# The expert part as one list of steps with a stated order, splits three groups ahead

## The chip, the cores and the metric

The kernel runs on one core of one Trainium2 chip. The metric is the device time of one execution in microseconds (us); less is better. Three runs of the kernel before gave 1487.68, 1487.93 and 1492.42 us.

## What is computed

A two-layer decoder trunk on 256 tokens of width 1024: attention and a dense SwiGLU, then a gated linear recurrence and a mixture of experts. The change touches the last part alone:

```
logits = t @ w_router                       # t: 256 x 1024 after RMSNorm, 8 experts
top_vals, top_idx = top_k(logits, 2); top_w = softmax(top_vals)
for e in range(8):                          # w_gate, w_up: 1024 x 3584; w_down: 3584 x 1024
    y = (silu(t @ w_gate[e]) * (t @ w_up[e])) @ w_down[e]
    out = out + gates[:, e:e+1] * y
```

All weights and results are float32. Each expert's weights are read once: 8 x 3 x 1024 x 3584 x 4 bytes, 352 MB.

## The kernel before

A float32 product is made of three fp32r matmuls: each operand is split into a high part and a low rest, and `mm3` (L100) adds high x high, high x low and low x high in PSUM (lines L101, L102, L103). The activations are split when they are made. The weights have to be split on the way: `load` (L82) brings 1 MB of weights into one of 14 `raw` buffers over SP's DMA queue, and `split` (L88) makes from each half of it `w_hi` on ACT (ACTIVATE, Copy) and then `w_lo` on DVE (raw minus `w_hi`). `w_hi` and `w_lo` have four buffers each (`NSUB` = 4). A split of 128x1024 elements feeds one group of six matmuls of 512 columns.

The experts are taken in pairs. For a pair, one-hot matrices (`one_hot`, L1084) pick up to 128 tokens for each of the two experts, `gather_pair` (L1111) gathers their rows by matmul into `xgh`/`xgl` (32 matmuls of 256 columns, evictions shared by ACT and DVE), and `pair_rows` makes gates and row numbers. An expert's 3584 hidden columns are done in seven jobs of 512 (class `Job`, L1134), 56 jobs in all. A job has four parts:

- `gate` (L1160): two loads, four splits, 24 matmuls into a PSUM bank `acc`, then Silu on ACT (`sg`, L1163)
- `up` (L1165): the same 24 matmuls with the other weights, then a product on DVE (`hm`, L1168)
- `turn` (L1170): four transposes of `hm` on PE into `tp` (L1173), then the high part `hh` on ACT (L1177) and the rest `hl` on DVE (L1178); `hh` and `hl` have one buffer each
- `down` (L1180): two loads, four splits, 24 matmuls into the two PSUM banks `pj`, which collect over the seven jobs of an expert

`run_jobs` (L1258) traces them in the order gate of job n, turn of job n-1, up of job n, down of job n-1. Ahead of a new pair (`fresh`) come the gather, with the turn of the last job in its middle, and the down of the last job. When an expert is done, `add` (L1194) scales `pj` by the gates on ACT (`y`, L1202) and an indirect DMA adds the rows to `out`; these steps wait in the list `later`, which `into` (L1144) works off after its splits. `FirstJob` (L1227) computes its gate for all tokens while the routing (`route`, L1026) is under way; `LastJob` (L1214) does its down in column halves so that the first half can leave early.

The order in which an engine executes its instructions is fixed when the program is built. A planner goes through the traced instructions with its own model of their times and puts an instruction on an engine when it reckons it ready; among ready ones the earlier traced goes first. `tc.issue_after(i)` adds an edge by which the instructions of a block come behind instruction `i` on `i`'s engine; it adds no wait between engines. In the kernel before, the expert part has such edges for the `y` steps alone; where splits, Silu, `hh`, `hl`, `hm`, transposes and matmuls stand against each other is the planner's choice. Each engine works through its own list in order.

Of the kernel before, what the change touches and what calls it, by code (L numbers as in the profile page):

```python
# [16 lines left out]
P = 128  # L17
D = 1024
KT = D // P
NT = 2  # L20
# [19 lines left out]
def tile_trunk(  # L40
# [59 lines left out]
    def mm3(ps, xh, xl, wh, wl, first, last, chk=False):  # L100
        nc.tensor.matmul(ps, lhsT=xh, rhs=wh, start=first, stop=False, skip_group_check=chk)  # L101
        nc.tensor.matmul(ps, lhsT=xh, rhs=wl, start=False, stop=False, skip_group_check=chk)  # L102
        nc.tensor.matmul(ps, lhsT=xl, rhs=wh, start=False, stop=last, skip_group_check=chk)  # L103
# [1007 lines left out]
    def gather_pair(oneh, between=None):  # L1111

        xg = slot_tiles(2 * P)
        for k0 in range(0, KT, 2):
            if k0 == 4 and between:
                between()
            for src, dst in ((nh, xg[0]), (nl, xg[1])):
                pt = bank("acc", 4)
                for i in range(2):
                    k = k0 + i  # L1120
                    for t in range(NT):
                        nc.tensor.matmul(pt[:, i * 256:(i + 1) * 256], lhsT=src[t][:, k * P:(k + 1) * P],
                                         rhs=oneh[:, t], start=(t == 0), stop=(t == NT - 1))
                pv = pt.rearrange("p (a b) -> p a b", b=256)
                if src is nh:
                    nc.scalar.activation(dst[:, k0:k0 + 2], pv, AF.Copy)
                else:
                    nc.vector.tensor_copy(dst[:, k0:k0 + 2], pv)
        return xg

    NCH = FE // 512
    later = []

    class Job:  # L1134
# [9 lines left out]
        def into(self, w):  # L1144
            rows = self.rows()
            ps = [bank("acc", 4) for _ in rows]
            for k0 in (0, 4):
                r = load([4, 512], lambda r: [(r, w[:, k0:k0 + 4, self.ch * 512:(self.ch + 1) * 512])])
                for i in range(0, 4, 2):
                    wh, wl = split(r[:, i:i + 2], [2, 512])  # L1150
                    for j in range(2):
                        k = k0 + i + j
                        for p_, (xh, xl, es) in zip(ps, rows):
                            mm3(p_, xh[:, k, es], xl[:, k, es], wh[:, j], wl[:, j], k == 0, k == KT - 1)
                    if later and k0 + i:
                        with tc.issue_after(split.last[0].ins):
                            later.pop(0)()
            return ps

        def gate(self):  # L1160
            ps, = self.into(self.wg)
            self.sg = moe.tile([P, 512], F32, name="sg", tag="sg", bufs=1)
            nc.scalar.activation(self.sg, ps, AF.Silu)  # L1163

        def up(self):  # L1165
            ps, = self.into(self.wu)
            self.hm = moe.tile([P, 512], F32, name="hm", tag="hm", bufs=1)
            nc.vector.tensor_mul(self.hm, ps, self.sg)  # L1168

        def turn(self):  # L1170
            pt = bank("tp")
            for i in range(4):
                nc.tensor.transpose(out=pt[:, i * P:(i + 1) * P], in_=self.hm[:, i * P:(i + 1) * P], identity=ident)  # L1173
            self.hh = moe.tile([P, 4, P], F32R, name="hh", tag="hh", bufs=1)
            self.hl = moe.tile([P, 4, P], F32R, name="hl", tag="hl", bufs=1)
            ptv = pt.rearrange("p (a b) -> p a b", b=P)
            nc.scalar.activation(self.hh, ptv, AF.Copy)  # L1177
            nc.vector.tensor_sub(self.hl, ptv, f32(self.hh))  # L1178

        def down(self):  # L1180
            sh, ch = self.shared, self.ch
            if ch == 0:
                sh["py"] = [bank("pj") for _ in range(2)]
            for i0 in (0, 2):
                r = load([2, D], lambda r: [(r, self.wd[:, 4 * ch + i0:4 * ch + i0 + 2, :])])
                for i in range(2):
                    wh, wl = split(r[:, i], [D])
                    for c in range(2):
                        mm3(sh["py"][c], self.hh[:, i0 + i], self.hl[:, i0 + i], wh[:, HALF[c]], wl[:, HALF[c]],
                            ch == 0 and i0 + i == 0, ch == NCH - 1 and i0 + i == 3)  # L1190
            if ch == NCH - 1:
                later.extend(self.add(0, 2, out_rows, 0))

        def add(self, c0, c1, rows, i):  # L1194

            (gate, idx), j, py = self.shared["slots"], self.slot, self.shared["py"]
            box = {}

            def scaled(c):
                if c == c0:  # L1200
                    box["y"] = lows.tile([P, 2, 512], F32, name="y", tag="low1")
                nc.scalar.activation(box["y"][:, c], py[c], AF.Copy, scale=gate[:, j:j + 1])  # L1202
                if c == c1 - 1:
                    out_of(box["y"])

            def out_of(y):
                nc.gpsimd.indirect_dma_start(
                    out=rows, out_offset=bass.IndirectOffsetOnAxis(ap=idx[:, i, j:j + 1], axis=0),
                    in_=y[:, c0:c1].rearrange("p a b -> p (a b)"), in_offset=None, bounds_check=rows.shape[0] - 1,
                    oob_is_err=True, compute_op=ALU.add)  # L1210

            return [lambda c=c: scaled(c) for c in range(c0, c1)]

    class LastJob(Job):  # L1214

        def down(self):
            sh = self.shared
            for c in range(2):
                for i0 in (0, 2):
                    r = load([2, 512], lambda r: [(r, self.wd[:, 4 * self.ch + i0:4 * self.ch + i0 + 2, HALF[c]])])  # L1220
                    wh, wl = split(r, [2, 512])
                    for i in range(2):
                        mm3(sh["py"][c], self.hh[:, i0 + i], self.hl[:, i0 + i], wh[:, i], wl[:, i], False, i0 + i == 3)
                for step in self.add(c, c + 1, out_halves, 1 + c):
                    step()

    class FirstJob(Job):  # L1227

        def gate(self):
            self.ch_rows = [(*dense, TOK[t]) for t in range(NT)]  # L1230
            self.sgh = lows.tile([P, NT, 512], F32R, name="sgh", tag="low1")
            self.sgl = []
            for t, ps in enumerate(self.into(self.wg)):
                sg = moe.tile([P, 512], F32, name="sg", tag=("sg", "hm")[t], bufs=1)
                nc.scalar.activation(sg, ps, AF.Silu, scale=rx[t])
                nc.scalar.activation(self.sgh[:, t], sg, AF.Copy)
                self.sgl.append(moe.tile([P, 512], F32R, name="sgl", tag=("hl", "hh")[t], bufs=1))
                nc.vector.tensor_sub(self.sgl[t], sg, f32(self.sgh[:, t]))
            self.ch_rows = None
# [4 lines left out]
        def up(self):  # L1244
            sh = self.shared
            sh["oneh"] = one_hot(0)
            sh["xg"] = gather_pair(sh["oneh"])
            sh["slots"] = pair_rows(sh["oneh"], 0)
            pt = bank("tp")
            for t in range(NT):  # L1250
                for n, part in enumerate((self.sgh[:, t], self.sgl[t])):
                    nc.tensor.matmul(pt, lhsT=sh["oneh"][:, t, 0], rhs=part, start=(t == 0 and n == 0),
                                     stop=(t == NT - 1 and n == 1))
            self.sg = moe.tile([P, 512], F32, name="sg", tag="sg", bufs=1)
            nc.scalar.activation(self.sg, pt, AF.Copy)
            super().up()

    def run_jobs(jobs):  # L1258

        prev = None  # L1260
        for job in jobs + [None]:
            if job and job.fresh:
                job.fresh(job.shared, prev.turn)
                prev.down()
                prev = None
            if job:
                job.gate()
            if prev:
                prev.turn()
            if job:  # L1270
                job.up()
            if prev:
                prev.down()
            prev = job

    jobs = []
    for e in range(NE):
        if e % 2 == 0:
            shared = {}

            def fresh(sh, between, e=e):
                sh["oneh"] = one_hot(e)
                sh["xg"] = gather_pair(sh["oneh"], between)
                sh["slots"] = pair_rows(sh["oneh"], e)
# [9 lines left out]
    run_jobs(jobs)  # L1294
# [7 lines left out]
    with tc.If(most > P):  # L1302
        ecur = mc.tile([P, 1], F32, name="ecur")
        nc.vector.memset(ecur, 0.0)
        with tc.For_i(0, NE, 1) as e:
# [27 lines left out]
            run_jobs([Job(ch, shared, slice(0, P), ws, 0) for ch in range(NCH)])  # L1333
            while later:
                later.pop(0)()
# [44 lines left out]
```

## Time and profile before

| | us |
|---|---|
| three runs: lowest, median, highest | 1487.68, 1487.93, 1492.42 |
| the profiled execution, its own time | 1489.99 |
| its span, first to last instruction | 1488.3 |
| PE busy, over the span | 1453.3 (98%) |
| DVE busy, over the span | 1213.9 (82%) |
| ACT busy, over the span | 1035.2 (70%) |
| first expert gather matmul | at 510.7 |
| down part of the first job begins | at 532.81 |
| down part of the last job but one begins | at 1464.62 |

How to read it: matmuls are pipelined, each row of PE lasts longer than the distance to the next, so PE shows as busy throughout and busy time doesn't tell whether it ran at its best. The distance from one start to the next does. PEld is the weight load of a matmul; its idle time has a releaser when it waited for another engine. A row of the timeline gives start, length, engine, line, operation, what it writes and reads, how many rows were merged, and in brackets the idle time just before it and what ended it.

### The profile page before, as it was taken

The page shows a single profiled execution, that of the slowest core. Times are in us where ns is not written, and L with a number is a line of the kernel's source. Part 1 is how long each engine was busy: PE and PEld are TensorE (multiplying, and loading weights), DVE is VectorE, ACT ScalarE, POOL GpSimd, SP SyncE. Part 2 cuts the span into 40 slices and gives each one's busy share as a digit, 9 for nine tenths or more (in the row PEclk, how much of TensorE's full clock was granted, in tenths as well). Part 3 has the DMA queues.
Part 4 walks back from the last instruction along what each step waited for, and adds up shares of the span by engine and source line. Part 5 has one row for each costly group of instructions (what it writes and reads, how often), then busy time and mean ns, then how long its engine had stood idle before and what let it go on. Part 6 is the DMA issues. An engine that isn't in the chain of part 4 may idle for free.

```text
span 1488.3 us, 20143 instructions
## 1 busy us (share of the span) xinstructions
PE 1453.3 (98%) x7509; PEld 1216.6 (82%) x7509; DVE 1213.9 (82%) x1460; ACT 1035.2 (70%) x1285; POOL 31.9 (2%) x45
## 2 busy tenths in 40 slices
PE   7999999999999999999999999999999999999996
PEld 6887899998889788888888878888877888887885
DVE  7775656557867899999989888889888888888885
ACT  6655544445766688888878777777777777778774
POOL 1000000000000100000000000000000000000000
PEclk9999999999999999999999999999999999999999
DMA  9933355656454499999999999999999999999971
GB/s 315 369 125 114 128 182 187 186 183 183 142 170 142 143 348 365 384 370 385 379 348 376 356 351 395 360 353 360 374 367 373 381 366 350 356 371 362 391 262 16
DMA packets 209691, 434.05 MB, mean 292 GB/s; under 512 B 7402, under 2 KB 58642, under 8 KB 209586
## 3 DMA queue, kind: packets, MB, share of 16 engines
q1 hardware_dynamic: 207506, 425.77, 79.6%
q0 software_dynamic: 2080, 6.92, 2.3%
q8 instruction: 61, 1.00, 0.3%
q14 instruction: 44, 0.36, 0.1%
HBM read 427.41 MB, written 5.24 MB: 291 GB/s over the span
## 4 chain that ended last, share of the span: by engine, by line
issue 53%; PE 37%; DMA 5%; DVE 2%; ACT 2%; POOL 0%; SPq 0%; POOLq 0%; ACTq 0%; DVEq 0%
PE acc L101 5%; PE acc L102 5%; PE acc L103 5%; DMA out_dram<-y,idx 4%; PE pj L342 3%; PE pj L344 3%; PE pj L343 3%; PE pj L101 2%; PE pj L103 2%; PE pj L102 2%; DVE w_lo L91 1%; PE pj L760 1%; PE pj L761 1%; PE pj L762 1%; PE tp L556 1%
## 5 line engine op out<-in xcount | busy, mean ns | idle before, releaser
L91 DVE TENSOR_TENSOR w_lo<-raw,w_hi 128x1024 fp32r<-128x1024 f32 x810 | 956.8, 1221 | 169.2 <-ACT w_hi L91 153.5
L91 ACT ACTIVATE w_hi<-raw 128x1024 fp32r<-128x1024 f32 x810 | 830.0, 1057 | 248.4 <-PE acc L103 82.9
L102 PE MATMUL acc<-w_lo,xgh 128*128 128x512 f32 x904 | 357.9, 396 | 0.0
L101 PE MATMUL acc<-w_hi,xgh 128*128 128x512 f32 x904 | 354.2, 392 | 1.0 <-ACT xgh L294 1.0
L103 PE MATMUL acc<-w_hi,xgl 128*128 128x512 f32 x904 | 353.2, 391 | 0.0
L102 PEld LDWEIGHTS acc<-w_lo,xgh 128*128 128x128 f32 x904 | 169.6, 188 | 51.8 <-DVE w_lo L91 14.6
L101 PEld LDWEIGHTS acc<-w_hi,xgh 128*128 128x128 f32 x904 | 169.8, 188 | 37.1 <-ACT xgh L294 1.2
L103 PEld LDWEIGHTS acc<-w_hi,xgl 128*128 128x128 f32 x904 | 169.8, 188 | 33.0
L102 PE MATMUL pj<-w_lo,hh 128*128 128x512 f32 x448 | 177.8, 397 | 0.0
L103 PE MATMUL pj<-w_hi,hl 128*128 128x512 f32 x448 | 174.9, 390 | 0.0
L101 PE MATMUL pj<-w_hi,hh 128*128 128x512 f32 x448 | 158.1, 391 | 0.7 <-ACT hh L1177 0.5
L101 PEld LDWEIGHTS pj<-w_hi,hh 128*128 128x128 f32 x448 | 84.1, 188 | 19.6 <-ACT hh L1177 0.9
L103 PEld LDWEIGHTS pj<-w_hi,hl 128*128 128x128 f32 x448 | 84.2, 188 | 16.3
L102 PEld LDWEIGHTS pj<-w_lo,hh 128*128 128x128 f32 x448 | 84.2, 188 | 16.3
L342 PE MATMUL pj<-xh,w_hi 128*128 128x256 f32 x320 | 90.8, 284 | 0.6 <-DVE hm L677 0.6
L343 PE MATMUL pj<-xl,w_hi 128*128 128x256 f32 x320 | 90.5, 283 | 0.0
L344 PE MATMUL pj<-xh,w_lo 128*128 128x256 f32 x320 | 90.5, 283 | 0.0
L1163 ACT ACTIVATE sg<-acc 128x512 f32<-128x512 f32 x55 | 32.9, 598 | 52.8 <-PE acc L103 52.8
L1177 ACT ACTIVATE hh<-tp 128x512 fp32r<-128x512 f32 x56 | 33.4, 596 | 49.8 <-PE pj L102 43.4
L342 PEld LDWEIGHTS pj<-xh,w_hi 128*128 128x128 f32 x320 | 61.4, 192 | 1.2 <-DVE hm L677 0.8
L343 PEld LDWEIGHTS pj<-xl,w_hi 128*128 128x128 f32 x320 | 61.4, 192 | 0.4
L344 PEld LDWEIGHTS pj<-xh,w_lo 128*128 128x128 f32 x320 | 61.4, 192 | 0.0
(300 smaller groups left out, 1594.3 us busy)
## 6 DMA issues: line engine op xcount, KB each, us to landing
raw<-in_moe_w_gate_dram SPq DMA_DIRECT2D x112, 1024.0 KB, 7.4
raw<-in_moe_w_up_dram SPq DMA_DIRECT2D x112, 1024.0 KB, 7.9
raw<-in_moe_w_down_dram SPq DMA_DIRECT2D x110, 1024.0 KB, 7.6
raw<-in_ffn_w_gate_dram SPq DMA_DIRECT2D x22, 512.0 KB, 3.8
raw<-in_ffn_w_up_dram SPq DMA_DIRECT2D x22, 512.0 KB, 4.8
raw<-in_ffn_w_down_dram SPq DMA_DIRECT2D x11, 1024.0 KB, 4.8
raw<-in_hgrn_w_in_dram SPq DMA_DIRECT2D x10, 1024.0 KB, 5.5
raw<-in_attn_w_in_dram SPq DMA_DIRECT2D x16, 512.0 KB, 9.3
```

The lines of the kernel that those rows point to most:

```text
L91: split.last = nc.scalar.activation(hi, view, AF.Copy), nc.vector.tensor_sub(lo, view, f32(hi))
L101: nc.tensor.matmul(ps, lhsT=xh, rhs=wh, start=first, stop=False, skip_group_check=chk)
L102: nc.tensor.matmul(ps, lhsT=xh, rhs=wl, start=False, stop=False, skip_group_check=chk)
L103: nc.tensor.matmul(ps, lhsT=xl, rhs=wh, start=False, stop=last, skip_group_check=chk)
L342: nc.tensor.matmul(o, lhsT=wh[:, i, j], rhs=xh[:, k], start=k == 0 and j == 0, stop=False, skip_group_check=True)
L343: nc.tensor.matmul(o, lhsT=wh[:, i, j], rhs=xl[:, k], start=False, stop=False, skip_group_check=True)
L344: nc.tensor.matmul(o, lhsT=wl[:, i, j], rhs=xh[:, k], start=False, stop=k == KT - 1, skip_group_check=True)
L556: nc.tensor.matmul(po[:, j * 64:(j + 1) * 64], lhsT=pT[:, kb, j, :], rhs=v[:, kb, j * 64:(j + 1) * 64], start=(j == 0 and kb == 0), stop=( ...
L760: nc.tensor.matmul(o, lhsT=wh[:, k], rhs=xh[:, k], start=first, stop=False, skip_group_check=True)
L761: nc.tensor.matmul(o, lhsT=wh[:, k], rhs=xl[:, k], start=False, stop=False, skip_group_check=True)
L1163: nc.scalar.activation(self.sg, ps, AF.Silu)
L1177: nc.scalar.activation(self.hh, ptv, AF.Copy)
```

## The change

The jobs no longer issue their work part by part. Each part returns a list of steps, `order` strings the lists of all jobs together in the same sequence as `run_jobs` did, and `run` issues the one list. A step is either a plain function or a `Split`, which has a load, a view of it, and `use`, the matmuls of the group. Before `run` issues the matmuls of a group it issues the splits up to three groups further (`AHEAD = NSUB - 1`), across the borders of parts and jobs. `tails` holds the last instruction issued on PE, ACT and DVE; `in_turn` puts every following split, group of matmuls, Silu, `hm`, `turn`, gather step and `y` behind these, each engine on its own. `one_hot` of a new pair is traced behind the gate of the last job before it, and `later` is worked off after every group. `FirstJob`'s own steps (apart from the gather), `one_hot`, `pair_rows` and the loads are in no such order. The number of matmuls, splits, loads and evictions, the tiles and the buffers stay as they are.

```diff
+    tails = {}
+    @contextmanager
+    def in_turn():
+        with ExitStack() as st:
+            for i in tails.values():
+                st.enter_context(tc.issue_after(i.ins))
+            yield
+    AHEAD = NSUB - 1
+    class Split:
+        def __init__(self, load_, view, shape, use):
+            self.load, self.view, self.shape, self.use = load_, view, shape, use
+        def ready(self):
+            with in_turn():
+                self.parts = split(self.view(self.load()), self.shape)
+            tails["act"], tails["dve"] = split.last
+    def run(steps):
+        splits = [x for x in steps if isinstance(x, Split)]
+        n = done = 0
+        for x in steps:
+            if not isinstance(x, Split):
+                x()
+                continue
+            while n < min(len(splits), done + AHEAD + 1):
+                splits[n].ready()
+                n += 1
+            with in_turn():
+                tails["pe"] = x.use(*x.parts)
+            done += 1
+            if later:
+                later.pop(0)()
...
         def into(self, w):
-            rows = self.rows()
-            ps = [bank("acc", 4) for _ in rows]
-            for k0 in (0, 4):
-                r = load([4, 512], lambda r: [(r, w[:, k0:k0 + 4, self.ch * 512:(self.ch + 1) * 512])])
-                for i in range(0, 4, 2):
-                    wh, wl = split(r[:, i:i + 2], [2, 512])
...
+            return [Split(ld, lambda r, i=i: r[:, i:i + 2], [2, 512], lambda wh, wl, k=k0 + i: use(k, wh, wl))
+                    for k0, ld in ((0, part(0)), (4, part(4))) for i in (0, 2)]
...
         def turn(self):
             pt = bank("tp")
+            with in_turn():
+                for i in range(4):
+                    tails["pe"] = nc.tensor.transpose(out=pt[:, i * P:(i + 1) * P], in_=self.hm[:, i * P:(i + 1) * P], identity=ident)
...
+                tails["act"] = nc.scalar.activation(self.hh, ptv, AF.Copy)
+                tails["dve"] = nc.vector.tensor_sub(self.hl, ptv, f32(self.hh))
...
+    def order(jobs):
+        steps, prev = [], None
+        for n, job in enumerate(jobs):
+            if job.fresh:
+                a, b = gather_steps(job.shared)
+                steps += [a, prev.turn, b, lambda job=job: job.fresh(job.shared)] + prev.down()
                 prev = None
+            steps += job.gate()
+            if n + 1 < len(jobs) and jobs[n + 1].fresh:
+                steps.append(jobs[n + 1].one_hot)
             if prev:
+                steps.append(prev.turn)
+            steps += job.up()
             if prev:
+                steps += prev.down()
             prev = job
+        return steps + [prev.turn] + prev.down()
```

## Rows read from the trace of the kernel before

**Rows 1.** Page, part 1: busy us, share of the span, instructions.

```profile
PE 1453.3 (98%) x7509; PEld 1216.6 (82%) x7509; DVE 1213.9 (82%) x1460; ACT 1035.2 (70%) x1285; POOL 31.9 (2%) x45
```

**Rows 2.** Busy us (instructions): PE, PEld, DVE, ACT, POOL; clock, DMA share, GB/s.

```profile
533.00:735.00 202.00, 202.00 (x915) 167.18 (x914) 187.55 (x169) 164.60 (x171) 1.69 (x1) 1.00 1.03 377
...
1259.00:1461.00 202.00, 202.00 (x900) 162.42 (x899) 178.75 (x166) 153.34 (x167) 1.83 (x1) 1.00 0.91 332
```

**Rows 3.** Timeline of PE: where six down parts, one gate and one turn begin.

```profile
532.81 0.39 PE L101 MATMUL pj<-w_hi,hh 128*128 128x512 f32 x1
...
555.06 0.39 PE L101 MATMUL acc<-w_hi,xgh 128*128 128x512 f32 x1
...
560.51 0.60 PE L1173 MATMUL tp<-ident,hm 128*128 128x128 f32 x4
...
734.45 0.39 PE L101 MATMUL pj<-w_hi,hh 128*128 128x512 f32 x1
...
772.33 0.39 PE L101 MATMUL pj<-w_hi,hh 128*128 128x512 f32 x1
...
839.79 0.62 PE L101 MATMUL pj<-w_hi,hh 128*128 128x512 f32 x2
...
856.92 0.61 PE L101 MATMUL pj<-w_hi,hh 128*128 128x512 f32 x2
...
1464.62 0.62 PE L101 MATMUL pj<-w_hi,hh 128*128 128x512 f32 x2
```

**Rows 4.** Timeline of ACT and DVE, one job of the early stretch.

```profile
560.71 0.60 ACT L1163 ACTIVATE sg<-acc 128x512 f32<-128x512 f32 x1 [0.31 <-PE acc L103]
561.20 0.59 ACT L1177 ACTIVATE hh<-tp 128x512 fp32r<-128x512 f32 x1
561.68 2.01 ACT L91 ACTIVATE w_hi<-raw 128x1024 fp32r<-128x1024 f32 x2
...
562.77 4.80 DVE L91 TENSOR_TENSOR w_lo<-raw,w_hi 128x1024 fp32r<-128x1024 f32 x4 [0.26 <-ACT w_hi L91]
...
567.49 0.68 DVE L1168 TENSOR_TENSOR hm<-acc,sg 128x512 f32<-128x512 f32 x1
```

**Rows 5.** Timeline of ACT, DVE and PE, one job of the later stretch.

```profile
897.27 0.60 ACT L1177 ACTIVATE hh<-tp 128x512 fp32r<-128x512 f32 x1 [1.45 <-PE pj L102]
...
902.95 0.60 ACT L1163 ACTIVATE sg<-acc 128x512 f32<-128x512 f32 x1 [1.30 <-PE acc L103]
...
904.53 3.50 DVE L91 TENSOR_TENSOR w_lo<-raw,w_hi 128x1024 fp32r<-128x1024 f32 x3 [1.05 <-ACT w_hi L91]
...
905.47 0.39 PE L101 MATMUL acc<-w_hi,xgh 128*128 128x512 f32 x1
905.81 0.50 PE L102 MATMUL acc<-w_lo,xgh 128*128 128x512 f32 x1
```

**Rows 6.** Waits of PEld, 822 to 1465; its groups by line, 549.6 to 734.4.

```profile
PEld acc L102 <- DVE w_lo L91: 14.6, 41, 0.4
...
L102 PEld LDWEIGHTS acc<-w_lo,xgh 128*128 128x128 f32 x176 | 33.1, 188 | 6.5
```

**Rows 7.** Timeline of ACT and PE behind the first gather between pairs.

```profile
743.86 0.60 ACT L1126 ACTIVATE xgh<-acc 128x512 fp32r<-128x512 f32 x1 [0.34 <-PE acc L1122]
...
744.51 0.48 PE L101 MATMUL pj<-w_hi,hh 128*128 128x512 f32 x1
```

**Rows 8.** Waits of SP's queue; DMA issues (KB, median us to landing), 533 to 735.

```profile
SPq L85 <- DVE w_lo L91: 171.0, 73, 3.3
...
raw<-in_moe_w_up_dram SPq DMA_DIRECT2D x24, 1024.0 KB, 8.1
```

**Rows 9.** Timeline of ACT and PE at the last turn.

```profile
1470.51 0.60 ACT L1177 ACTIVATE hh<-tp 128x512 fp32r<-128x512 f32 x1 [1.44 <-PE pj L102]
...
1471.16 0.50 PE L101 MATMUL pj<-w_hi,hh 128*128 128x512 f32 x1 [0.46 <-ACT hh L1177]
```

**Rows 10.** Timeline of PE at the first gather.

```profile
510.70 0.39 PE L1122 MATMUL acc<-oneh,nh 128*128 128x256 f32 x1 [1.30 <-DVE oneh L1087]
```

More of the change, by code (lines that the diff above doesn't have):

```diff
@@ L102, in mm3 @@
         nc.tensor.matmul(ps, lhsT=xh, rhs=wl, start=False, stop=False, skip_group_check=chk)
-        nc.tensor.matmul(ps, lhsT=xl, rhs=wh, start=False, stop=last, skip_group_check=chk)
+        return nc.tensor.matmul(ps, lhsT=xl, rhs=wh, start=False, stop=last, skip_group_check=chk)
     def pair_load(w, c0, c1, k):
@@ L1109, in pair_rows @@
         return slot_rows(lambda t, j: oneh[:, t, j], lambda t, j: info[:, t, e + j], 2)
[L1111 to L1129, printed above, removed]
+    tails = {}
@@ L1170, in turn, with out_ @@
+        def up(self):
+            def out_():
+                self.hm = moe.tile([P, 512], F32, name="hm", tag="hm", bufs=1)
+                with in_turn():
+                    tails["dve"] = nc.vector.tensor_mul(self.hm, self.ps[0], self.sg)
+            return self.into(self.wu) + [out_]
         def turn(self):
             pt = bank("tp")
-            for i in range(4):
-                nc.tensor.transpose(out=pt[:, i * P:(i + 1) * P], in_=self.hm[:, i * P:(i + 1) * P], identity=ident)
@@ L1191, in down, with use, part @@
-            if ch == NCH - 1:
-                later.extend(self.add(0, 2, out_rows, 0))
+            def use(i, wh, wl):
+                if ch == 0 and i == 0:
+                    sh["py"] = [bank("pj") for _ in range(2)]
+                for c in range(2):
+                    m = mm3(sh["py"][c], self.hh[:, i], self.hl[:, i], wh[:, HALF[c]], wl[:, HALF[c]],
+                            ch == 0 and i == 0, ch == NCH - 1 and i == 3)
+                return m
+            def part(i0):
+                return once(lambda: load([2, D], lambda r: [(r, self.wd[:, 4 * ch + i0:4 * ch + i0 + 2, :])]))
@@ L1194, in add @@
+            steps = [Split(ld, lambda r, i=i: r[:, i], [D], lambda wh, wl, i=i0 + i: use(i, wh, wl))
+                     for i0, ld in ((0, part(0)), (2, part(2))) for i in range(2)]
+            return steps + ([lambda: later.extend(self.add(0, 2, out_rows, 0))] if ch == NCH - 1 else [])
         def add(self, c0, c1, rows, i):
@@ L1216, in down, with use, leave @@
         def down(self):
-            sh = self.shared
+            sh, steps = self.shared, []
+            def use(c, i0, wh, wl):
+                for i in range(2):
+                    m = mm3(sh["py"][c], self.hh[:, i0 + i], self.hl[:, i0 + i], wh[:, i], wl[:, i], False, i0 + i == 3)
+                return m
+            def leave(c):
+                for step in self.add(c, c + 1, out_halves, 1 + c):
+                    step()
             for c in range(2):
                 for i0 in (0, 2):
[L1220 to L1225, printed above, removed]
+                    ld = once(lambda c=c, i0=i0: load([2, 512], lambda r: [
+                        (r, self.wd[:, 4 * self.ch + i0:4 * self.ch + i0 + 2, HALF[c]])]))
+                    steps.append(Split(ld, lambda r: r, [2, 512], lambda wh, wl, c=c, i0=i0: use(c, i0, wh, wl)))
+                steps.append(lambda c=c: leave(c))
+            return steps
     class FirstJob(Job):
@@ L1245, in up, with ready @@
             sh = self.shared
[L1246 to L1264, printed above, removed]
+            def ready():
+                sh["oneh"] = one_hot(0)
+                for step in gather_steps(sh):
+                    step()
+                sh["slots"] = pair_rows(sh["oneh"], 0)
+                pt = bank("tp")
+                for t in range(NT):
+                    for n, part in enumerate((self.sgh[:, t], self.sgl[t])):
+                        nc.tensor.matmul(pt, lhsT=sh["oneh"][:, t, 0], rhs=part, start=(t == 0 and n == 0),
+                                         stop=(t == NT - 1 and n == 1))
+                self.sg = moe.tile([P, 512], F32, name="sg", tag="sg", bufs=1)
+                nc.scalar.activation(self.sg, pt, AF.Copy)
+            return [ready] + super().up()
+    def order(jobs):
[4 more added lines that the diff above has]
+                steps += [a, prev.turn, b, lambda job=job: job.fresh(job.shared)] + prev.down()
                 prev = None
-            if job:
-                job.gate()
+            steps += job.gate()
+            if n + 1 < len(jobs) and jobs[n + 1].fresh:
+                steps.append(jobs[n + 1].one_hot)
             if prev:
-                prev.turn()
-            if job:
-                job.up()
+                steps.append(prev.turn)
+            steps += job.up()
             if prev:
-                prev.down()
+                steps += prev.down()
             prev = job
+        return steps + [prev.turn] + prev.down()
     jobs = []
@@ L1279, in tile_trunk, with fresh, hot @@
             shared = {}
[L1281 removed]
+            def fresh(sh, e=e):
+                sh["slots"] = pair_rows(sh["oneh"], e)
+            def hot(sh=shared, e=e):
                 sh["oneh"] = one_hot(e)
[L1283 to L1284 removed]
             if e == 0:
@@ L1293, in tile_trunk @@
                 fresh if e in (2, 4, 6) and ch == 0 else None))
-    run_jobs(jobs)
+            jobs[-1].one_hot = hot
+    run(order(jobs))
     cmax = mc.tile([P, 1], F32, name="cmax")
@@ L1332, in tile_trunk @@
             shared = dict(xg=xg2, slots=slot_rows(lambda t, j: oh2[:, t], lambda t, j: info2[:, t], 1))
-            run_jobs([Job(ch, shared, slice(0, P), ws, 0) for ch in range(NCH)])
-            while later:
-                later.pop(0)()
+            tails.clear()
+            run(order([Job(ch, shared, slice(0, P), ws, 0) for ch in range(NCH)]))
             nc.vector.tensor_scalar(ecur, ecur, 1.0, None, op0=ALU.add)
```

99 lines of the change are left out of this document (61 added, 38 removed).

## The prediction, made before the change was run

> **What bounds the kernel now.** I read the page's busy times first. PE shows 98% [rows 1], and in the expert part it shows as busy in every microsecond, at the full clock: the granted clock is 1.00 of full speed, the 2.4 GHz level, in both stretches [rows 2]. So PE sets the time there. But overlapping matmul rows hide small losses, so the next view is the timeline of PE, read by distances between starts. A gate part has 24 matmuls from 555.06 to 560.51 [rows 3]: 5.45 / 24 = 0.227 us from one to the next, without a break. A job has 72 of them, 16.34 us, and four transposes.
>
> Then I mark where each job's down part begins and compare the distances. From 532.81 to 734.45 there are twelve jobs [rows 3], 201.64 / 12 = 16.80 us each: 0.46 us above the 72 matmuls, which the transposes account for. From 839.79 to 856.92 it is 17.13 [rows 3]. So the same work runs in two ways, an early one (A) and a later one (B), and B loses about 0.3 us in each job.
>
> The waits of PEld say where: from 822 to 1465 it waited for `w_lo` 41 times, 14.6 us in all, and for nothing else; in A its weight loads of the same line have idle time but no releaser [rows 6]. One such wait is the step from 905.47 to 905.81 [rows 5], 0.34 us instead of 0.227.
>
> Last I read ACT and DVE in both. In A a job's order on ACT is Silu, `hh`, then the splits, and Silu waits 0.31 us [rows 4]; DVE does four `w_lo` before `hm`. In B the planner put `hh` before a split, although the one `hh` buffer is read by the running down part to its end: ACT stands 1.45 us until that frees it, and Silu then stands 1.30 us [rows 5]. The splits queued behind come late, DVE stands 1.05 us for `w_hi` [rows 5], and PE waits for that `w_lo`. This is a matter of order; the buffers, instructions and durations are the same in A and B.
>
> **The change, part by part.**
>
> *The list's order.* I set the list of steps against the A rows. Before the last gate group the splits up to the third group of up are issued; then Silu, the transposes, `hh`, `hl`; then the last split of up, then those of down. On ACT that gives Silu, `hh`, then splits, and on DVE `hl`, four `w_lo`, `hm`: the order of rows 4. In A every split also starts when the group before the one now running has freed its buffer, which is three groups ahead with four buffers. So the list is A for all jobs, and A's pace needs no estimate. The edges are on one engine each and cost no instruction.
>
> The price: from 532.81 to 1464.62 [rows 3] the kernel takes 931.81 us. There are 54 distances from one down part to the next; six of them lie at the three gathers between pairs, two at each. In A these two take 772.33 - 734.45 = 37.88 us [rows 3]. All in A: 48 x 16.803 + 3 x 37.88 = 806.5 + 113.6 = 920.2 us. **The gain is 931.8 - 920.2 = 11.6 us**, all of it on PE's path. A larger gain isn't there: the whole of PEld's wait is 14.6 us.
>
> *Waits in the new order.* A split that is released late now holds all that is behind it. The tightest place is the Silu: behind it stand `hh` and the last split of up. Silu starts 0.31 us after ACT fell idle, `hh` 0.49 us later, the split 0.48 us later [rows 4]; PE needs that split three groups of 1.36 us and the transposes after the gate's end at 560.51 [rows 3], at about 564.9. Its `w_lo` begins at 562.77 and takes 1.2 us [rows 4], so it is there at 564.0. That leaves 0.9 us of cover, and A shows no wait.
>
> *The loads* are issued at a split's place in the list, so up to three groups earlier in the program. They are in none of the orders; SP has been ahead by its 14 buffers anyway: it waited 171 of 202 us for a free buffer, and a load lands 8.1 us after its issue [rows 8]. Cost nothing; their cover is the lead of 14 buffers, 14 x 2.8 = 39 us of PE work at six loads to a job, less 8.
>
> *Gathers between pairs.* The list puts the last split of a job's down behind all evictions; the kernel before had it ahead of them. The last `xgh` eviction starts at 743.86 and takes 0.60 us [rows 7]. So in the list the split starts at about 744.5, its `w_lo` is ready 2.3 us later, at 746.8, and PE, which begins that down part at 744.51 [rows 7], comes to it three groups later, at 748.6. Cost nothing with 1.8 us of cover; without it up to 1 us at each of three places. `one_hot` and `pair_rows` float as before.
>
> *First job.* PE stands 1.30 us until the one-hot matrix is there [rows 10], at the end of DVE's routing work. The splits of up now precede `one_hot` in the program, but four buffers let at most three of them come early, and three have done so before. No row shows the new place: at best the 1.30 us goes, at worst three `w_lo` of 1.2 us [rows 4] come in front (3.6 us). I take 0, since the same three splits stand there before.
>
> *The end.* The last turn now follows the last but one down in full. Before, the first matmul behind that turn starts at 1471.16, 6.54 us after 1464.62 [rows 3, 9]. Now: 24 matmuls 5.44, transposes to `hh` 0.69 (560.51 to 561.20 [rows 3, 4]), `hh` to matmul 0.65 [rows 9], 6.78 us; against that, the wait for a late split that followed goes, as three are ready. I take 0, with -0.6 to +0.8.
>
> *A rule against the trace.* PE's pace in A is 0.227 us a matmul with no wait beside it [rows 3, 6]. The Trainium skill (TensorE: Matmul & The Clock Gate, section "Wait — 56ns, not 53.3ns?") has 215.7 ns from start to start for 512 columns at the full clock. By that figure a job would have 0.8 us less, and the gain would be some 45 us more; the trace doesn't agree, and the measured pace stands.
>
> **The sum.** -11.6 us. The profiled execution took 1489.99 us (its span is 1488.3), the median of the runs 1487.93, 2.06 us less. 1489.99 - 11.6 = 1478.4 as a profiled run, 1476.3 against the median, 0.8% faster.
>
> **The rivals.**
>
> *New waits eat half.* The unordered rest (`one_hot`, `pair_rows`, the first job's steps) or the gather borders add waits: 3.6 us at the first job, 1 us at each gather, together 6.6 us; 1482.9. Against it: the first gather shows no wait in nearly the same order. 8%.
>
> *It doesn't do what it says.* The planner's order stays where it matters, or the wait returns at another place in the job: 1487.9. For it speaks only that edges add order and no speed; against it that each of the instructions that stand wrongly in rows 5 is tied. 6%.
>
> *The transfers become the bound; slower.* Now DMA moves 377 GB/s in A at a share of 1.03 [rows 2], which looks full. If the core can't hold that for the rest, the 31 us of lead are used up. The point of decision: 56 jobs of 6.29 MB, less the lead, end no earlier than 931.8 + 31 us if the rate is 366 GB/s; below that the kernel is slower than before, at 355 GB/s by 992 - 963 = 29 us, 1517. Against it: landing takes 8 of 39 us, and SP waits for buffers, not for data [rows 8]. The Trainium skill (Perfetto Trace Analysis, section "Identifying the Most-Contended Engine") calls occupancy misleading for the 16 DMA engines and goes by HBM utilization; by that the share of 1.03 would be no sign of a bound, and the rows agree. 4%.
>
> *More than A.* The 1.30 us at the first job and the wait at the end go too: 1474. 4%. *The pace of the matmuls falls too*: a weight load takes 0.188 us [rows 6], so 0.227 might hold something that an order frees; each 0.01 us is 40 us in 4032 matmuls, and one such step gives 1436. No stretch of A shows it: 1%.
>
> **How the numbers follow.** The forecast gets 77%. A measurement of this kernel tells about 0.3%, 4.5 us, from no change. Faster by more than that are the forecast, the half (5.0 us), more and the pace: 77 + 8 + 4 + 1 = 90%, of which I move 2% to no change, since the half lies near the bound: 88%. Same: 6 + 2 = 8%. Slower: 4%. The range goes from 1473 (all of the bounds for the first job and the end below the forecast, 1.9 us, and the runs' spread) to 1482 (the first job's 3.6 us, the end's 0.8, and a run from the upper part of a spread of 4.7 us); it leaves out the transfers, no change and most of the half.
>
> **What would show it.** Right: down parts 16.8 us apart up to the last gather, no wait of PEld for `w_lo`, Silu and `hh` back to back on ACT in every job, DVE with four `w_lo` before `hm`, the last down but one beginning near 1453. Wrong: distances of 17.1 that stay, ACT waits of 1.3 us for Silu or `hh`, ACT waiting for `raw` or landings above 30 us (transfers), a longer wait than 1.30 us ahead of the first gather, distances over 38 us at the gathers. The prediction falls as a whole if the tied order turns out to differ from rows 4 in a place that these rows do not show.

## The result, and the profile after

The changed kernel takes 1476.61 us (median of six runs, 1475.87 to 1481.65), the kernel before 1487.93 us on the same chip: a ratio of 0.9918 with a 95% interval of 0.9903 to 0.9933, or 11.3 us less. The profiled execution took 1475.87 us, with a span of 1474.2 us.

The page's busy times can't show it; PE still stands at 98%, as in [rows 1]:

```profile
PE 1439.5 (98%) x7509; PEld 1220.1 (83%) x7509; DVE 1231.7 (84%) x1460; ACT 1059.0 (72%) x1285; POOL 32.5 (2%) x45
```

The distances do. PE's timeline of the changed kernel (start, us; duration, us; what): the first gather, the first down part, the fourth group of one at the first gather between pairs, two down parts in a row of the later stretch, the last but one, and the first matmul behind the last turn.

```profile
508.25 0.38 PE L1133 MATMUL acc<-oneh,nh 128*128 128x256 f32 x1 [1.30 <-DVE oneh L1087]
...
530.52 0.39 PE L101 MATMUL pj<-w_hi,hh 128*128 128x512 f32 x1
...
746.42 0.39 PE L101 MATMUL pj<-w_hi,hh 128*128 128x512 f32 x1
...
887.66 0.39 PE L101 MATMUL pj<-w_hi,hh 128*128 128x512 f32 x1
...
904.47 0.39 PE L101 MATMUL pj<-w_hi,hh 128*128 128x512 f32 x1
...
1450.71 0.39 PE L101 MATMUL pj<-w_hi,hh 128*128 128x512 f32 x1
...
1457.44 0.50 PE L101 MATMUL pj<-w_hi,hh 128*128 128x512 f32 x1 [0.69 <-ACT hh L1239]
```

The later stretch has 904.47 - 887.66 = 16.81 us to a job where [rows 3] has 17.13, and so has every other job down to the end; the two distances at each gather between pairs sum to 37.85, 37.85 and 37.84 us. From the first down part to the last but one it is 1450.71 - 530.52 = 920.19 us, against 931.81 in [rows 3]: 11.6 us less. Between 515 and 1455 us PEld now waits for nothing at all, where [rows 6] has 41 waits.

ACT and DVE, a job of the later stretch (this answers to [rows 5]), and three rows of ACT and DVE at the first gather between pairs:

```profile
742.07 1.05 ACT L91 ACTIVATE w_hi<-raw 128x1024 fp32r<-128x1024 f32 x1
743.34 1.22 DVE L91 TENSOR_TENSOR w_lo<-raw,w_hi 128x1024 fp32r<-128x1024 f32 x1
...
898.74 0.60 ACT L1219 ACTIVATE sg<-acc 128x512 f32<-128x512 f32 x1 [0.30 <-PE acc L103]
899.23 0.59 ACT L1239 ACTIVATE hh<-tp 128x512 fp32r<-128x512 f32 x1
899.71 2.01 ACT L91 ACTIVATE w_hi<-raw 128x1024 fp32r<-128x1024 f32 x2
...
900.80 4.83 DVE L91 TENSOR_TENSOR w_lo<-raw,w_hi 128x1024 fp32r<-128x1024 f32 x4 [0.25 <-ACT w_hi L91]
905.55 0.68 DVE L1227 TENSOR_TENSOR hm<-acc,sg 128x512 f32<-128x512 f32 x1
```

It is the order of [rows 4], to within 0.01 us: Silu 0.30 us after ACT fell idle, `hh` 0.49 us later, four `w_lo` before `hm`. ACT's waits from 533 to 1455 us (us in total, times, longest) say the same of all jobs:

```profile
ACT sg L1219 <- PE acc L103: 16.3, 54, 0.3
...
ACT hh L1239 <- PE tp L1235: 0.9, 3, 0.3
```

Two stretches, as in [rows 2] (busy us of PE, PEld, DVE, ACT, POOL; clock, DMA share, GB/s):

```profile
533.00:735.00 202.00, 202.00 (x915) 167.19 (x914) 187.75 (x170) 164.46 (x171) 1.96 (x1) 1.00 1.02 376
1245.00:1447.00 202.00, 202.00 (x915) 167.21 (x914) 187.52 (x169) 164.67 (x172) 1.82 (x1) 1.00 0.92 339
```

SP's queue, 533 to 735 us, as in [rows 8]:

```profile
SPq L85 <- DVE w_lo L91: 169.1, 72, 3.3
```

The loads of up there (KB, us to landing):

```profile
raw<-in_moe_w_up_dram SPq DMA_DIRECT2D x24, 1024.0 KB, 7.2
```

The late stretch now holds 915 matmul records in 202 us like the early one, where [rows 2] has 900. The two profiled spans differ by 14.1 us, more than the medians do; 2.4 us of that lie before 150 us, in code that the change leaves alone, where the two executions just differ: PE's last transposes ahead of the routing begin at 488.17 us here and at 490.59 us before.

### The profile page after: what moved, and what is told of

The parts are those of the page before. It is cut to its first block, busy times and chain, and to the rows that moved or that the text cites. A ratio compares the mean times of both kernels' runs of the same rounds, so it can differ in the third digit from the quotient of the medians.

```text
span 1474.2 us, 20073 instructions
## 1 busy us (share of the span) xinstructions
PE 1439.5 (98%) x7509; PEld 1220.1 (83%) x7509; DVE 1231.7 (84%) x1460; ACT 1059.0 (72%) x1285; POOL 32.5 (2%) x45
## 4 chain that ended last, share of the span: by engine, by line
issue 61%; PE 29%; DMA 5%; DVE 2%; ACT 2%; POOL 0%; SPq 0%; POOLq 0%; ACTq 0%; DVEq 0%
DMA out_dram<-y,idx 4%; PE acc L101 3%; PE acc L102 3%; PE acc L103 3%; PE pj L342 3%; PE pj L344 3%; PE pj L343 3%; PE pj L101 1%; PE pj L103 1%; PE pj L102 1%; PE pj L760 1%; PE pj L761 1%; PE pj L762 1%; DVE w_lo L91 1%; PE tp L556 1%
## 5 line engine op out<-in xcount | busy, mean ns | idle before, releaser
L91 DVE TENSOR_TENSOR w_lo<-raw,w_hi 128x1024 fp32r<-128x1024 f32 x810 | 975.1, 1223 | 156.6 <-ACT w_hi L91 116.9
L91 ACT ACTIVATE w_hi<-raw 128x1024 fp32r<-128x1024 f32 x810 | 853.5, 1062 | 299.7 <-PE acc L103 127.5
L102 PE MATMUL acc<-w_lo,xgh 128*128 128x512 f32 x904 | 352.4, 390 | 0.0
L102 PE MATMUL pj<-w_lo,hh 128*128 128x512 f32 x448 | 174.3, 389 | 0.0
L101 PE MATMUL pj<-w_hi,hh 128*128 128x512 f32 x448 | 163.5, 390 | 0.7 <-ACT hh L1239 0.7
L101 PE MATMUL acc<-w_hi,xh 128*128 128x512 f32 (+1 forms) x160 | 58.7, 368 | 1.5 <-ACT xh L294 0.8
L102 PE MATMUL acc<-w_lo,xh 128*128 128x512 f32 (+1 forms) x160 | 57.6, 361 | 0.0
```

The source lines that it names most:

```text
L91: split.last = nc.scalar.activation(hi, view, AF.Copy), nc.vector.tensor_sub(lo, view, f32(hi))
```

## The experiments

In all of them "distance" is that between the starts of two down parts in a row, and "first to last" the time from the first to the last but one; the changed kernel has 16.80 and 920.19 us.

**Lead.** The list changes two things at once: the place of the turn and of Silu, and the lead of the splits, three groups ahead of PE. These two kernels keep the list and take the lead away.

```diff
-    AHEAD = NSUB - 1
+    AHEAD = NSUB - 2
```

(ahead1 has `NSUB - 3`.)

> The changed kernel with splits issued two groups ahead instead of three; all order edges stay. Theory of place (the one of the prediction: what cost time was that hh and Silu stood too early on ACT): both still stand back to back behind the gate, so the distance between down parts stays 16.8 us and the time 1476 to 1478. Theory of lead (what cost time was that only two split groups were ready when ACT came to the Silu, so that the third one's w_lo came too late): the third split of up now stands behind Silu and hh, its w_lo is there 3.5 us after the start of the transposes and PE wants it at 0.36 + 2 x 1.36 + 0.23 = 3.3 us, so every job waits for w_lo once, some 0.3 us as before the change: distance 17.1, time 1476 + 54 x 0.3 = 1492.

> The changed kernel with splits issued one group ahead; all order edges stay. Theory of lead: at the Silu the second split of up is late by 3.5 - 0.36 - 1.36 - 0.23 = 1.6 us, and at hm the second split of down by about 0.45 us, so each job loses 2.0 us: distance 18.9, time about 1476 + 110 = 1586. Theory of place: no loss at the Silu, since its place and that of hh are unchanged; only the 0.45 us at hm, distance 17.3, time about 1500.

Two groups ahead: ratio 1.0012 (1.0002 to 1.0023), so the whole gain is gone; distances 17.05 to 17.10 us, first to last 934.4 us. One group ahead, in one run: 1591.9 us, distances 18.83 to 18.88. PE, ACT and DVE of one job of the kernel with two groups ahead show the order to be right and the loss to be there:

```profile
889.81 0.60 ACT L1219 ACTIVATE sg<-acc 128x512 f32<-128x512 f32 x1 [1.66 <-PE acc L103]
890.30 0.59 ACT L1239 ACTIVATE hh<-tp 128x512 fp32r<-128x512 f32 x1
890.78 4.90 ACT L91 ACTIVATE w_hi<-raw 128x1024 fp32r<-128x1024 f32 x5
...
891.87 4.63 DVE L91 TENSOR_TENSOR w_lo<-raw,w_hi 128x1024 fp32r<-128x1024 f32 x4 [0.25 <-ACT w_hi L91]
...
892.79 0.39 PE L101 MATMUL acc<-w_hi,xgh 128*128 128x512 f32 x1
893.15 0.50 PE L102 MATMUL acc<-w_lo,xgh 128*128 128x512 f32 x1
893.49 0.39 PE L103 MATMUL acc<-w_hi,xgl 128*128 128x512 f32 x1
```

Its waits of PEld (us in total, times, longest):

```profile
PEld acc L102 <- DVE w_lo L91: 20.9, 55, 0.4
```

One wait in each job, and always this one. The chain from Silu to the first `w_lo` is the same as in the changed kernel: 889.81 to 891.87 is 2.06 us, and so is 898.74 to 900.80. What differs is which group that `w_lo` is for. With three ahead it is the fourth group of up, with two ahead the third, which PE reaches 1.36 us sooner. It is ready at 891.87 + 1.2 = 893.1, and the weight load that waits for it would run beside the matmul of 892.79. So PE goes 0.36 and 0.34 us where 0.227 is its pace: 0.25 us lost, the whole of the longer distance.

**The turn's place.** The rival was that the place makes the gain: `hh` and Silu no longer stand in front of splits while they wait. Here the turn is put where ACT must stand for it, right behind the previous job's down, with three groups ahead as before, and then with two.

```diff
-                steps += [a, prev.turn, b, lambda job=job: job.fresh(job.shared)] + prev.down()
+                steps += [a] + ([] if prev.turned else [prev.turn]) + [b, lambda job=job: job.fresh(job.shared)] + prev.down()
...
-                steps += prev.down()
+                steps += prev.down() + [job.turn]
```

(late_turn2 has `AHEAD = NSUB - 2` on top.)

> The changed kernel with the turn of a job moved from behind the next gate to behind the down of the job before, so that on ACT hh stands ahead of the next gate's last split and waits for the end of that down, as it did in the slow stretch before the change; three groups ahead and all edges stay. Theory of place: ACT stands for hh in every job again, distance 17.1 and time 1487 to 1490. Theory of lead: three split groups are ready when ACT gets there and the split behind hh still comes 1 us early, distance 16.8, time 1475 to 1479.

> The changed kernel with the turn moved as in late_turn and splits two groups ahead: the two things that rows of the slow stretch before the change show together. Theory of lead: the slow stretch again, one wait of PEld for w_lo in each job, at the third group of up; distance 17.0 to 17.1, time 1488 to 1492. If place and lead add up: distance 17.3 or more, since Silu and hh each hold the splits at a place of their own, time above 1500.

With three ahead: 0.9917 (0.9901 to 0.9934), the same gain; first to last 921.1 us, where the 0.9 us more lie at the gathers (PEld waits 0.8 us there for `xgh`). ACT and PE of one job:

```profile
896.36 0.60 ACT L1239 ACTIVATE hh<-tp 128x512 fp32r<-128x512 f32 x1 [0.74 <-PE tp L1235]
896.85 2.00 ACT L91 ACTIVATE w_hi<-raw 128x1024 fp32r<-128x1024 f32 x2
...
901.85 0.60 ACT L1219 ACTIVATE sg<-acc 128x512 f32<-128x512 f32 x1 [0.30 <-PE acc L103]
...
907.09 0.62 PE L101 MATMUL pj<-w_hi,hh 128*128 128x512 f32 x2
...
923.88 0.61 PE L101 MATMUL pj<-w_hi,hh 128*128 128x512 f32 x2
```

ACT's wait for the turn, 533 to 1455 us:

```profile
ACT hh L1239 <- PE tp L1235: 37.7, 51, 0.7
```

ACT stands 37.7 us for `hh`, in 51 jobs, and the distance is 923.88 - 907.09 = 16.79 us. So standing in front of splits costs nothing here: the lead covers it. With two ahead, one run: 1501.9 us, distances of 17.27 to 17.32 (one in each pair 17.40 to 17.44), and the waits come twice in a job:

```profile
PEld acc L102 <- DVE w_lo L91: 38.0, 111, 0.4
```

Place and lead draw on the same cover: either fault alone costs 0 (place) or 0.26 us (lead), both together 0.5 us a job.

**The edges.** Does the list need them, or does writing the steps in this order do? And does tying the turn alone do?

```diff
-            for i in tails.values():
-                st.enter_context(tc.issue_after(i.ins))
```

> The changed kernel without the edges: the steps are traced in the same sequence with splits three groups ahead, but the planner may put them in another order. If the edges do the work: the planner falls back into the late order, with transposes in the middle of a down part and waits of PEld for w_lo, 1484 to 1488. If the sequence in which the steps are traced is enough: 1475 to 1478 and no such wait.

Ratio 1.002 (1.0009 to 1.0031), first to last 933.8 us. The distances are 16.80 up to the fourth job behind the first gather between pairs, and 17.1 from there: the place where the kernel before changes from A to B. ACT and PE of one such job:

```profile
887.11 0.60 ACT L1217 ACTIVATE sg<-acc 128x512 f32<-128x512 f32 x1 [1.30 <-PE acc L103]
887.60 4.91 ACT L91 ACTIVATE w_hi<-raw 128x1024 fp32r<-128x1024 f32 x5
...
889.97 0.50 PE L102 MATMUL acc<-w_lo,xgh 128*128 128x512 f32 x1
```

It is the sight of [rows 5]: Silu stands 1.30 us on an ACT that has no split left to do before it, then five splits in a row, and a `w_lo` matmul that comes late. Without edges the planner orders this program much as it ordered the one before.

One part of the change alone is the kernel before with its turn tied behind the next gate's last matmul and Silu:

```diff
+            self.silu = nc.scalar.activation(self.sg, ps, AF.Silu)
...
-            if prev:
+            if prev and job:
+                with tc.issue_after(job.mm.ins), tc.issue_after(job.silu.ins):
+                    prev.turn()
+            elif prev:
```

> The kernel before, with one thing of the change: the four transposes of a turn come behind the last matmul of the next gate on PE, and hh behind that gate's Silu on ACT. Splits, matmuls, Silu and hm stay with the planner, and nothing is traced ahead. If the early transposes and hh were what led the planner into the late order: distances of 16.8 throughout, no wait for w_lo, 1476 to 1479. If the splits ahead are needed: distances near 17.1 return, 1485 to 1490.

Ratio 1.0076 (1.0057 to 1.0095): slower than the kernel before, with distances of 17.45 to 17.53 in the later stretch, 944.2 us from first to last, and waits in two places:

```profile
PEld pj L102 <- DVE w_lo L91: 17.0, 33, 0.5
PEld acc L102 <- DVE w_lo L91: 14.9, 39, 0.8
```

A tied turn with splits that still float is worse than all floating, so the turn's edges alone don't carry the gain. A kernel with the edges of the splits alone was not run.

**More lead.** Five split buffers and four groups ahead; 13 load buffers instead of 14 make the room.

```diff
-NRAW = 14
-NSUB = 4
+NRAW = 13
+NSUB = 5
```

> The changed kernel with five w_hi/w_lo buffers and splits four groups ahead (13 raw buffers instead of 14, to make room). If PE is the bound with three groups ahead, more lead gives nothing: distance 16.8, 1475 to 1478. If a wait that no row shows is left in the pace of 0.227 us a matmul, a longer lead shortens it: distance below 16.7, 1470 or less.

Ratio 0.9954 (0.9941 to 0.9967): faster than the kernel before, but not as fast as with three. The distances are 16.80, and the first gather between pairs takes no longer than before. The second and third take 12.19 + 27.72 = 39.91 us instead of 37.85, together 4.1 us, which is all of 924.3 - 920.2 us. PE's longest wait from 515 us on says at what:

```profile
PE acc L1133 <- DVE xgl L1140: 2.6, 2, 1.3
```

DVE at the second gather says why:

```profile
983.30 0.17 DVE L1099 COPY sv<-tp 128x8 f32<-128x8 f32 x1 [4.30 <-PE tp L1096]
...
983.58 2.36 DVE L91 TENSOR_TENSOR w_lo<-raw,w_hi 128x1024 fp32r<-128x1024 f32 x2
985.86 1.28 DVE L1140 CAST xgl<-acc 128x512 fp32r<-128x512 f32 x2
```

`sv` is the first DVE step of `pair_rows`, which the list ties to nothing. Here the planner has put it ahead of two splits and of all `xgl` evictions of the gather: DVE stands 4.30 us until PE, in the middle of the gather, has made its input, then does the two splits, and PE waits for the buffers that the evictions free. At the third gather it is the same, 4.30 us. At the first gather, and at all three in the changed kernel, `sv` comes behind the last eviction and DVE doesn't stand for it:

```profile
982.63 0.15 DVE L1099 COPY sv<-tp 128x8 f32<-128x8 f32 x1
```

So what stands in the way is a step without a stated order. What four groups ahead would cost with `pair_rows` tied was not run. A further 1 us or so of the difference between the two ratios lies within their intervals.

**The transfers.** Half the load buffers, one run:

```diff
-NRAW = 14
+NRAW = 7
```

> The changed kernel with 7 raw buffers instead of 14. If the transfers have room, 7 x 2.8 = 19.6 us of lead against a landing of 7.5 us is still enough: distance between down parts 16.8 in the expert part (the parts before it share the buffers and may take longer). If the transfers are near their limit at 374 GB/s, the shorter lead shows: ACT waits for raw, distances above 17, 1490 or more.

1477.5 us, first to last 920.18 us. SP's queue, 533 to 735 us:

```profile
SPq L85 <- DVE w_lo L91: 169.4, 72, 3.3
```

The loads of up there:

```profile
raw<-in_moe_w_up_dram SPq DMA_DIRECT2D x24, 1024.0 KB, 8.1
```

With half the lead a load still lands in 8.1 us, and SP waits for buffers as long as before.

**The pace.** This kernel leaves out all loads and splits of weights but the first of each shape, and uses those again for all groups (12 load buffers instead of 14 make the room).

```diff
-            with in_turn():
-                self.parts = split(self.view(self.load()), self.shape)
-            tails["act"], tails["dve"] = split.last
+            key = tuple(self.shape)
+            if key not in kept:
...
+            self.parts = kept[key]
```

> The changed kernel without nearly all loads and splits of the expert weights: only the first of each shape is loaded and split, and all groups use these two pairs (so the output is not the reference's); matmuls, transposes, Silu, hm, hh and hl stay. ACT, DVE and DMA have little to do. If 0.227 us from one matmul to the next is PE's own pace for these matmuls, the distance stays 16.8 and the time near 1476. If the pace suffers from what DVE, ACT and DMA do beside it, it falls towards 0.216 us, distance 16.0, about 1430.

1482.3 us in one run, first to last 926.6, distances of 16.92 us. Its stretch from 560 to 730 us:

```profile
560.00:730.00 170.00, 170.00 (x766) 139.76 (x765) 14.13 (x21) 12.24 (x22) 1.69 (x1) 1.00 0.02 4
```

DVE and ACT idle for more than nine tenths and the transfers gone, PE does 766 instructions where the changed kernel does 770. So I see nothing left in 16.80 us that an order of the splits could take. Why this kernel is even 0.12 us a job slower stays open; the excess lies in all matmuls alike, (16.92 - 0.46) / 72 = 0.229 us, neither PE nor PEld shows a wait in its jobs, and I have no run that tells the cause.

**The two ends.** Two small waits are left: 1.30 us at the first gather, and at the end the second half of the last `y`, which starts 5.95 us after the first since it uses its buffer again. First the end alone: the second half in `sg`'s buffer, which is free by then. Then the first job too: up's third split is held back until the one-hot matrix is there.

```diff
-                    box["y"] = lows.tile([P, 2, 512], F32, name="y", tag="low1")
+                    box["y"] = (moe.tile([P, 1, 512], F32, name="y2", tag="sg", bufs=1) if i == 2 else
+                                lows.tile([P, 2, 512], F32, name="y", tag="low1"))
...
+    held = [6]
...
-            while n < min(len(splits), done + AHEAD + 1):
+            while n < min(len(splits), done + AHEAD + 1, *held):
...
                 sh["oneh"] = one_hot(0)
+                held.clear()
```

> The changed kernel with a buffer of its own for the second half of the last y (that of sg, which is free by then). In the trace after the change this y waits 5.26 us for the DMA of the first half, whose buffer it shares; its matmuls are done 3.0 us before it starts. If the buffer is what it waits for: it starts 3.0 us earlier and the end comes 3 us earlier, 1473.5. If the two indirect DMAs into out are kept apart anyway: the second is issued when the first has landed, at most 1.0 us earlier, 1475.6.

> As two_y, and in the first job the third split of up is issued behind the one-hot matrix instead of ahead of it. In the trace after the change its w_lo (1.14 us of DVE) stands in the middle of the routing work, and PE stands 1.30 us for the one-hot matrix. If that split is what delays it: the gather begins 1.1 us earlier, 1472.4 with the gain of two_y. If the routing chain waits for PE or ACT there: no change against two_y.

ACT and POOL at the end of the first of them:

```profile
1463.80 0.69 ACT L1271 ACTIVATE y<-pj,gate 128x512 f32<-128x512 f32 x1 [2.44 <-PE pj L103]
1466.52 0.69 ACT L1271 ACTIVATE y<-pj,gate 128x512 f32<-128x512 f32 x1 [2.03 <-PE pj L103]
...
1464.77 1.54 POOL L1276 DMA_INDIRECT out_dram<-y,idx  x1 [100.96 <-ACT y L1271]
1470.45 1.54 POOL L1276 DMA_INDIRECT out_dram<-y,idx  x1 [4.14 <-ACTq L1391]
```

`y` does come earlier, 2.72 us after the first, but the second store is issued 5.68 us after the first, where the changed kernel has 5.95: 0.27 us gained, not the 3.2 us that the early `y` offers. My theory that the buffer is what it waits for fell. A store takes 4.9 us from its issue to its landing there, so the second is issued about 0.8 us behind the landing of the first (1464.77 + 4.9 = 1469.7). In the second kernel the trace names that landing as what ended POOL's idle time, with the first store issued at 1460.75:

```profile
1466.46 1.54 POOL L1277 DMA_INDIRECT out_dram<-y,idx  x1 [4.16 <-DMA out_dram<-y,idx]
```

The ratio of the first is 0.9930 (0.9913 to 0.9946). With the split held back as well, 0.9923 (0.9906 to 0.9939), and PE's row at the first gather:

```profile
507.12 0.39 PE L1133 MATMUL acc<-oneh,nh 128*128 128x256 f32 x1 [0.21 <-DVE oneh L1087]
```

From the last transposes ahead of the routing (488.05 us) that is 19.07 us instead of 20.08, and the first down part begins 0.9 us sooner. Both are real in the trace and too small for the times: by these no version beats the changed kernel.

## Why the prediction was right, step by step

**The sum held, and by its own term.** 1476.3 us was forecast, 1476.6 measured; the expert part was to take 920.2 us and took 920.19. That A's pace needs no estimate is borne out: 16.80 us for all jobs, and 37.85 us at a gather for the 37.88 that I had from one.

**The order is A's.** Every sign that the prediction named is there: Silu and `hh` back to back, four `w_lo` before `hm`, no wait of PEld, the last but one down part at 1450.71 (near 1453, less the 2.4 us by which this execution ran ahead).

**The reason for B's loss was only half right.** I put it down to the places of `hh` and Silu on ACT, with the splits late behind them. late_turn has ACT stand for `hh` in every job without loss, and ahead2 has the right places with B's loss. What decides is how many groups are split when ACT comes to the Silu: three carry PE over it, two don't. B has this fault too: in [rows 5] the wait before 905.81 comes 12 matmuls, two groups, behind the gate's end (905.47 - 12 x 0.227 = 902.75, 0.20 us before Silu), so it is for the third group of up, as in ahead2. The place of `hh` costs next to nothing in that job. DVE and PE of the kernel before, behind `hh`:

```profile
898.85 4.63 DVE L91 TENSOR_TENSOR w_lo<-raw,w_hi 128x1024 fp32r<-128x1024 f32 x4 [0.26 <-ACT w_hi L91]
...
900.01 0.39 PE L101 MATMUL acc<-w_hi,xgh 128*128 128x512 f32 x1
900.24 0.40 PE L102 MATMUL acc<-w_lo,xgh 128*128 128x512 f32 x1
```

The first `w_lo` behind `hh` is for the third group of the gate and ready at 898.85 + 1.2 = 900.05, and PE goes from 900.01 to 900.24 at its pace. B's distance of 17.13 is near ahead2's, with one wait in a job, and not near late_turn2's, with two. The prediction had the lead, as a cover of 0.9 us at the tightest place. Read from the changed kernel it is 1.1 us: that `w_lo` is ready at 900.80 + 1.2 = 902.0, and its weight load, one matmul ahead of its own, runs at 903.11:

```profile
903.11 0.19 PEld L102 LDWEIGHTS acc<-w_lo,xgh 128*128 128x128 f32 x1
```

Less one group, 1.36 us, this is a lack of 0.26 us, and ahead2 lost 0.26 us a job. So the size of the cover was nearly right, and of the two places that I named only Silu's counts, since it settles how many groups are split before it. The sum held all the same: it takes A's measured pace and needs no cause.

**The terms that I took as nothing.** The gathers: the split that I expected behind the evictions at 744.5 (742.1, less the same 2.4 us) started at 742.07; its `w_lo` is ready at 743.34 + 1.22 = 744.6, and PE begins that group at 746.42. That is 1.9 us of cover, and I had 1.8. ahead4 breaks at this place, not by the split but by `pair_rows`, which the prediction let float as before. That it costs nothing in the changed kernel is the planner's choice and not secured by the change, so this term was in part luck. The first job: the wait for the one-hot matrix is 1.30 us as in [rows 10], and from the last transposes to the first down part 42.35 us instead of 42.22, so 0.1 us where I took 0 of a range to 3.6. The end: from the last but one down part to the matmul behind the last turn 6.73 us (I had 6.78), and to the end of the span 23.4 us instead of 23.7.

**The rivals.** That new waits eat half falls with the row of PEld's waits, which is empty. That the change doesn't do what it says falls with no_edges: without the edges the time goes back, and at the same job. The transfers are no bound: raw7 has the same pace with half the lead, no_split is no faster without them, and the share of 1.02 at 376 GB/s is no sign of one. That agrees with the Trainium skill (Perfetto Trace Analysis, section "Identifying the Most-Contended Engine"), by which occupancy misleads for the DMA engines; the HBM utilization that it goes by instead was not worked out here. That the pace of the matmuls falls too is out: it is 0.227 us in the changed kernel, and 0.229 us with everything beside PE nearly gone. That more than A comes of it was half there, 0.9 us at the first job and 0.27 us at the end, but only by edits that this change doesn't make.

## What to carry to other kernels

Where one engine is the bound and others prepare its input in queues that run in order, count at the worst place of the loop how many prepared pieces lie ahead of it, and how long the chain is from the event that holds the queue to the next piece; the lead in pieces times their time must exceed that chain, and one piece too few shows as a small wait in every turn of the loop. Such a loss hides in a busy share of 98% and shows in distances between like points; the early, undisturbed stretch of the same trace gives the price of mending it. More lead than that brought nothing here, and in that kernel the planner put a step without a stated order where it cost 2 us at each of two gathers: after such a change look again at whatever still floats.

## What the runs showed of the hardware

A matmul of 512 columns with a weight load of its own went every 0.227 us at a granted clock of 1.00 (the 2.4 GHz level), and in no_split, with a DMA share of 0.02 and DVE and ACT at under a tenth, still every 0.229 us. The 215.7 ns that the prediction took from the Trainium skill (TensorE: Matmul & The Clock Gate, section "Wait — 56ns, not 53.3ns?") were the pace of no run.

Two indirect stores into the same tensor, from two buffers, went one after the other: 5.68 us apart, with 4.9 us from issue to landing (the median of the two), though the second one's data was there 3.2 us before its issue. The row at 1466.46 names the landing of the first as what released the second, 0.8 us before its issue; what the chip does with two such stores where nothing waits, no run shows.

With 14 load buffers and with 7 the loads ran at the same pace, and the landing of up's loads took 7.2 and 8.1 us; so a share of 1.02 was not the sign of a limit that the expert part ran into.
